# A two-layer trunk of attention and MLP blocks on one core: layer norms by ScalarE, gains in transposed form, and the next stage's first 512 columns by halves of the tokens

## The chip, the cores and the metric

One core of a Trainium2 chip runs the whole program. The metric is device time in microseconds, from a launch to its end. Engines: TensorE (PE in the rows; PEld is its loading of weights), VectorE (DVE), ScalarE (ACT), GpSimd (POOL), and SyncE (SP), whose queue issues most transfers.

## What is computed

256 tokens of 2048 features pass through two layers, each an attention block and an MLP, each followed by a layer norm over a scaled residual:

```python
def layer_norm(x, g, b):
    mu = mean(x); var = mean((x - mu) ** 2)
    return (x - mu) * rsqrt(var + 1e-5) * g + b

def sq_relu_mlp(x, w1, w2):
    return square(relu(x @ w1)) @ w2

for layer in range(2):
    if layer == 0: mix = fox_attention(h, ...)       # 16 heads, forget gates
    else:          mix = nsa_attention(h, ..., *kv)  # compressed, selected and window branches
    h = layer_norm(ALPHA * h + mix, ln1_g[layer], ln1_b[layer])
    h = layer_norm(ALPHA * h + sq_relu_mlp(h, ...), ln2_g[layer], ln2_b[layer])
    if layer == 0: kv = shared_kv(h, kv_w, ...)      # 6 blocks of 512 columns
```

The weights are float32, 419 MB of them in the stream; 2048 by 8192 and back in each MLP, 2048 by 2048 for the attention's projections.

## The kernel before

**Layout.** `h` holds the tokens on partitions: two halves t = 0, 1 of 128 tokens, by 2048 columns; `c` or `n` is a block of 512 of them. A product needs its input with the features on partitions, so each norm's result is transposed on TensorE (L376, 128x128 at a time, into a PSUM tile `pt`) and copied out into `act` chunks.

**Float32 in two parts.** Each operand is split into a hi part, rounded to fp32r (a cast on ScalarE, L117), and a lo part, the remainder (a subtraction on VectorE, L118); a product takes hi x hi, hi x lo and lo x hi. `wload` brings 0.5 MB of weights into a `raw` tile (four of them) and splits it into a `whl` tile of 128 x 2 x 1024 (five of them). `fill_split` does the same for activations.

**Two forms of product.** The column form (`ws_many`, called by `ws_stream`) has 128 output features on partitions and all 256 tokens in a row: for each column j and each of 16 feature blocks one matmul 512 wide (L158, hi weights by hi and lo tokens) and one 256 wide (L160, lo weights by hi tokens). The row form (`xs_mm`, called by `xs_part`) has 128 tokens on partitions and 512 columns in a row, three matmuls 512 wide for each feature block and half (L182). MLPs read `w1` in the column form and `w2` in the row form; projections out of attention use the row form.

**Stages and handovers.** Fox attention, its output projection and norm 0; MLP 0 and norm 1; the shared kv blocks and NSA attention, its projection and norm 2; MLP 1 and norm 3, which is the output. Between a norm and the next product lies a handover, three of them: into MLP 0, into the kv blocks, into MLP 1. `out_proj` does the blocks n = 0 to 2 and hands back `end`, which does the last one. There the last LATE = 4 weight tiles are held in a pool `late`, so that all of t = 0's held matmuls (24) run before t = 1's (24). `done` adds a finished block to `h` (L248 or L250) and takes its statistics (L252). `scalars` makes mean and 1/sqrt(var) out of them in small VectorE operations (L321 to L328) around one square root on ScalarE (L324); L330 is for the last norm alone.

**The norm.** `gained` subtracts the mean and multiplies by the gains (L348), `columns` multiplies by 1/sqrt(var) and adds the bias (L363), both on VectorE in pieces of 256 columns, with gains and biases spread over all partitions (`lng`, `lnb`, 1 MB each, loaded into `late`). `transposer` transposes and splits. While t = 1's chain runs, TensorE does WARM = 14 dummy matmuls (L423) at the second and third handover; at the first it makes tables for the NSA stage (`tables`, L597 and L600) instead. What follows the chain stands inside `tc.issue_after(last)`: every engine gets it behind `last`, the final one of t = 1's scalars, in its order. The last norm has two of its pieces on ScalarE (L354) and GpSimd (L355, L356).

The next stage then begins in the column form, with three columns together in MLP 0, MLP 1 and the kv stream (`together` = 3), so that feature blocks can be multiplied as they come. The order of the instructions on each engine is worked out when the kernel is built, from the order of the code, priorities and the tiles that are free; TensorE, VectorE and ScalarE each work off their own list, and a transfer on SP waits for its tile.

Of the kernel before, what the change touches and what calls it, by code (L numbers as in the profile page):

```python
# [14 lines left out]
OP = mybir.AluOpType  # L15
# [17 lines left out]
LATE = 4  # L33
WARM = 14
# [64 lines left out]
def _trunk(nc, tc, i, out, ctx):  # L99
# [91 lines left out]
    def merge(dst, acc, scale=1.0):  # L191

        t = sp.tile([P, S], F32, tag="mt", name="mt")
# [41 lines left out]
    def out_proj(src, acts, first, ln=None, two=False, between=()):  # L235
# [41 lines left out]
        def end(late, meanwhile=None):  # L277

            ln.gains(late)
            accs = [acc_tile(), acc_tile()]  # L280
            ahead = 8 - LATE
# [5 lines left out]
            ws = [wload(src[3, k // 2], k % 2, late, LATE) for k in range(ahead, 8)]  # L287
            for t in range(2):
# [12 lines left out]
            elif not ln.final:  # L301
                warm(WARM, ws[0][:, 0, :P], ws[0][:, 0, :512])
            with tc.issue_after(last):
                for t, c in ln.rest:
                    ln.columns(t, c)
                if after:
                    after()
        return end

    class Norm:  # L310


        def __init__(self, li, use, final=False):
            self.li, self.use, self.sc, self.had, self.final = li, use, {}, set(), final
            self.early = (2, 3, 0, 1) if final else (0,)
            self.rest = ((1, 3), (1, 0), (1, 1), (1, 2)) if final else (
                (1, 0), (0, 1), (1, 1), (0, 2), (1, 2), (0, 3), (1, 3))

        def scalars(self, t):
# [8 lines left out]
            end = nc.vector.tensor_mul(rstd, y, a)  # L328
            if self.final:
                end = nc.vector.scalar_tensor_tensor(a, mean, -1.0, rstd, op0=OP.mult, op1=OP.mult)  # L330
# [3 lines left out]
        def gains(self, pool):  # L334
            self.gb = []
            for name in ("lng", "lnb"):
                x = pool.tile([P, D], F32, name=name, bufs=1)
# [3 lines left out]
        def pieces(self, t, c):  # L341
            n = 512 if self.final else 256
            return [[x[:, a:a + n] for x in (h[:, t], *self.gb)] for a in range(c * 512, (c + 1) * 512, n)]

        def gained(self, t, c):
            self.had.add((t, c))
            for hs, g, _ in self.pieces(t, c):
                nc.vector.scalar_tensor_tensor(hs, hs, self.sc[t][0], g, op0=OP.subtract, op1=OP.mult)  # L348

        def columns(self, t, c):  # L350
            mean, rstd, nmr = self.sc[t]
            if self.final and (c == 3 or (t, c) == (0, 2)):
                hs, g, b = (x[:, c * 512:(c + 1) * 512] for x in (h[:, t], *self.gb))
# [6 lines left out]
            if (t, c) not in self.had:  # L360
                self.gained(t, c)
            for hs, _, b in self.pieces(t, c):
                nc.vector.scalar_tensor_tensor(hs, hs, rstd, b, op0=OP.mult, op1=OP.add)  # L363
            self.use(t, c)
            if self.final and (t, c) == self.rest[-1]:
                self.use(1, 3)

    def transposer(cs):

        def use(t, c):  # L370
            if not cs:
                cs.extend(act_chunk() for _ in range(4))
            tp = pt_tile()
            for k in range(4):
                f = c * 512 + k * P
                nc.tensor.transpose(tp[:, k * P:(k + 1) * P], h[:, t, f:f + P], eye)  # L376
            for k in (0, 2):
                hi, lo = (cs[c][:, k:k + 2, n, t * P:(t + 1) * P] for n in range(2))
                fill_split(hi, lo, tp[:, k * P:(k + 2) * P].rearrange("p (k t) -> p k t", k=2))
        return use  # L380
# [4 lines left out]
    def mlp(layer, acts, ln):  # L385
        for q in range(4):
            hid = []

            def use(j, acc):
                if j % 4 == 0:  # L390
                    hid.append(act_chunk())
                u = sp.tile([P, S], F32, tag="mu", name="mu")
# [4 lines left out]
            ws_stream([i["w1"][layer, q * 16 + j] for j in range(16)], acts, use, 3 if q == 0 else 1)  # L397
            end = out_proj(i["w2"][layer, q], hid, q == 0, ln if q == 3 else None)
        with tc.tile_pool(name="late", bufs=2) as late:
            end(late)  # L400
# [16 lines left out]
    cb = cp.tile([P, 2, NC, H], F32, name="cb")  # L417

# [21 lines left out]
    def forget_gates():  # L440

        f = sp.tile([P, 5, 2, H], F32, name="f", bufs=1)
# [16 lines left out]
    def gate_sums():  # L459
# [8 lines left out]
        cr_sb = sp.tile([H, S], F32, name="cr", bufs=1)  # L468
# [3 lines left out]
    with tc.tile_pool(name="fp", bufs=2) as fp:  # L472
# [75 lines left out]
        for hg in range(G):  # L548
# [10 lines left out]
            if hg == 0:  # L559
                load(cst, i["cst"])  # L560
                load(bfb, i["bf"].to_broadcast([P, H]))
                gates_end()
# [22 lines left out]
        end = out_proj(i["fo"], oc, True, Norm(0, transposer(xs)), True, [lambda k=k: run(k) for k in range(n, n + 3)])  # L585

    with tc.tile_pool(name="late", bufs=2) as late:
# [23 lines left out]
        end(late, tables)  # L611
    acts, xs = xs, []
    mlp(0, acts, Norm(1, transposer(xs)))


    with tc.tile_pool(name="np", bufs=2) as np_:
# [22 lines left out]
        raws = ap.tile([P, 2, G, S], F32, tag="act", name="rawT")  # L639

        def use_raw(j, acc):
            merge(raws[:, j // G, j % G, :], acc)

        ws_stream([i["kvT"][s, g] for s in range(2) for g in range(G)], xs, use_raw, 3)
        gates_end = narrow(i["ng"], 3 * H, xs, C["s48"], gate)

        def windows(s):
            t = ap.tile([P, NB, 60], F32, tag="act", name="win")
            src = raws[:, s]
# [89 lines left out]
        def plain_v(s, steps=()):  # L739
            accs = [acc_tile(), acc_tile()]  # L740
            for kc in range(4):
                xs_part(i["kvN"][s, kc], xs[kc], accs, kc == 0, kc == 3)
                if kc < len(steps):
                    steps[kc]()
# [185 lines left out]
```

## Time and profile before

| | us |
|---|---|
| median of 3 runs | 2247.69 |
| lowest and highest | 2247.38, 2249.09 |
| the profiled execution, its own time | 2248.41 |
| its span, from the first to the last instruction | 2246.6 |

TensorE's mean granted clock in that execution is 0.995 of full speed. The span is what the trace shows; about 1.8 us lie around it. A row of the timeline gives a start, a duration, the engine, the line, the operation and how many instructions are merged in it; in brackets the idle time ahead of it and what ended that. Matmuls overlap in their pipeline, so time per matmul is read from one start to the next, not from the durations. Times are in microseconds from the start of the span.

### The profile page before, as it was taken

The page shows a single profiled execution, that of the slowest core. Times are in us where ns is not written, and L with a number is a line of the kernel's source. Part 1 is how long each engine was busy: PE and PEld are TensorE (multiplying, and loading weights), DVE is VectorE, ACT ScalarE, POOL GpSimd, SP SyncE. Part 2 cuts the span into 40 slices and gives each one's busy share as a digit, 9 for nine tenths or more (in the row PEclk, how much of TensorE's full clock was granted, in tenths as well). Part 3 has the DMA queues.
Part 4 walks back from the last instruction along what each step waited for, and adds up shares of the span by engine and source line. Part 5 has one row for each costly group of instructions (what it writes and reads, how often), then busy time and mean ns, then how long its engine had stood idle before and what let it go on. Part 6 is the DMA issues. An engine that isn't in the chain of part 4 may idle for free.

```text
span 2246.6 us, 30144 instructions
## 1 busy us (share of the span) xinstructions
PE 2220.6 (99%) x11478; PEld 1893.7 (84%) x11478; DVE 1408.0 (63%) x2209; ACT 1048.2 (47%) x1564; POOL 18.6 (1%) x26
## 2 busy tenths in 40 slices
PE   9999999999999999999999999999999999999997
PEld 6888888888888888888788899888888888888885
DVE  5665556864665565565786688768655645655655
ACT  4444444443444454454355567544434434444542
POOL 0000000000000000000000000000000000000001
PEclk9999999999999999999999999999999999999999
DMA  7665567566666666666556744565666666666663
GB/s 253 196 197 188 178 188 249 198 190 192 192 191 192 193 188 195 190 188 194 179 165 221 246 134 137 168 217 170 192 192 190 191 193 194 189 193 191 189 196 112
DMA packets 116829, 427.54 MB, mean 190 GB/s; under 512 B 13179, under 2 KB 13339, under 8 KB 115406
## 3 DMA queue, kind: packets, MB, share of 16 engines
q1 hardware_dynamic: 114734, 419.00, 59.5%
q0 software_dynamic: 1952, 6.63, 1.0%
q8 instruction: 90, 1.47, 0.3%
q14 instruction: 53, 0.43, 0.1%
HBM read 423.45 MB, written 4.24 MB: 190 GB/s over the span
## 4 chain that ended last, share of the span: by engine, by line
PE 95%; DVE 2%; DMA 2%; ACT 0%; issue 0%; SPq 0%; ACTq 0%; DVEq 0%
PE acc L182 44%; PE acc L158 31%; PE acc L160 16%; DMA raw<-in_fq 1%; PE pt L839 1%; PE lg L775 0%; PE pt L817 0%; PE pt L376 0%; DMA raw<-in_fv 0%; DVE whl L118 0%; DMA bc<-c_dram 0%; DVE h L363 0%; PE acc L692 0%; PE pt L840 0%; PE pt L533 0%; PE lg L771 0%
## 5 line engine op out<-in xcount | busy, mean ns | idle before, releaser
L118 DVE TENSOR_TENSOR whl<-raw,whl 128x1024 fp32r<-128x1024 f32 (+1 forms) x769 | 938.4, 1223 | 613.6 <-ACT whl L117 605.0
L117 ACT CAST whl<-raw 128x1024 fp32r<-128x1024 f32 (+1 forms) x769 | 805.1, 1048 | 740.3 <-PE acc L182 491.6
L182 PE MATMUL acc<-whl,act 128*128 128x512 f32 x4416 | 1011.7, 390 | 2.2 <-DVE whl L118 1.2
L182 PEld LDWEIGHTS acc<-whl,act 128*128 128x128 f32 x4416 | 827.1, 188 | 177.6 <-DVE whl L118 2.8
L158 PE MATMUL acc<-act,whl 128*128 128x512 f32 x3072 | 757.3, 394 | 0.0
L158 PEld LDWEIGHTS acc<-act,whl 128*128 128x128 f32 x3072 | 563.5, 189 | 107.3 <-issue 0.2
L160 PEld LDWEIGHTS acc<-act,whl 128*128 128x128 f32 x3072 | 398.2, 191 | 16.9 <-DVE whl L118 0.3
L160 PE MATMUL acc<-act,whl 128*128 128x256 f32 x3072 | 408.7, 284 | 0.0
L194 ACT ACTIVATE mt<-acc 128x256 f32<-128x256 f32 x192 | 73.4, 382 | 299.7 <-PE acc L158 297.5
L196 DVE TENSOR_TENSOR mu<-acc,mt 128x256 f32<-128x256 f32 x128 | 54.4, 425 | 113.4 <-ACT mt L194 113.4
L394 DVE SCALAR_TENSOR_TENSOR mu<-mu 128x256 f32<-128x256 f32 x128 | 54.4, 425 | 4.3
L118 DVE TENSOR_TENSOR act<-mu,act 128x256 fp32r<-128x256 f32 x128 | 53.7, 420 | 0.0
L117 ACT CAST act<-mu 128x256 fp32r<-128x256 f32 x128 | 52.1, 407 | 3.1 <-DVE mu L394 1.6
L117 ACT CAST act<-pt 128x256 fp32r<-128x256 f32 x80 | 29.4, 372 | 41.9 <-PE pt L376 31.3
L250 DVE TENSOR_TENSOR h<-h,acc 128x512 f32<-128x512 f32 x48 | 30.9, 681 | 14.2 <-PE acc L182 14.2
L118 DVE TENSOR_TENSOR act<-pt,act 128x256 fp32r<-128x256 f32 x80 | 33.1, 419 | 9.9 <-ACT act L117 9.6
L404 ACT ACTIVATE E<-E,sm 128x128 f32<-128x128 f32 (+1 forms) x64 | 28.9, 453 | 7.8 <-DVE sm L407 7.4
L363 DVE SCALAR_TENSOR_TENSOR h<-h,mv,lnb 128x256 f32<-128x256 f32 (+1 forms) x53 | 26.5, 541 | 0.1
L404 ACT ACTIVATE E<-L,sm 128x128 f32<-128x128 f32 (+1 forms) x32 | 14.3, 449 | 24.8 <-DVE sm L407 24.8
L376 PE MATMUL pt<-cst,h 128*128 128x128 f32 x96 | 19.1, 293 | 6.0 <-DVE h L363 6.0
L348 DVE SCALAR_TENSOR_TENSOR h<-h,mv,lng 128x256 f32<-128x256 f32 (+1 forms) x53 | 25.0, 502 | 0.0
L248 DVE SCALAR_TENSOR_TENSOR h<-h,acc 128x512 f32<-128x512 f32 x32 | 20.6, 681 | 4.2 <-PE acc L182 4.2
(173 smaller groups left out, 664.0 us busy)
## 6 DMA issues: line engine op xcount, KB each, us to landing
raw<-in_w SPq DMA_DIRECT2D x512, 512.0 KB, 3.6
raw<-in_fq SPq DMA_DIRECT2D x32, 512.0 KB, 3.7
raw<-in_fk SPq DMA_DIRECT2D x32, 512.0 KB, 3.6
raw<-in_fo SPq DMA_DIRECT2D x32, 512.0 KB, 4.0
raw<-in_kvT SPq DMA_DIRECT2D x32, 512.0 KB, 4.4
raw<-in_nq SPq DMA_DIRECT2D x32, 512.0 KB, 3.7
raw<-in_no SPq DMA_DIRECT2D x32, 512.0 KB, 4.1
raw<-in_fv SPq DMA_DIRECT2D x31, 512.0 KB, 3.7
```

The source lines that it names most:

```text
L117: nc.scalar.copy(hi, src)
L118: nc.vector.tensor_sub(lo, src, hi.bitcast(F32))
L158: mm(acc, w[:, 0, s], a, start=kt == 0, stop=kt == KT - 1)
L160: mm(acc[:, :S], w[:, 1, s], a[:, 0, :], start=False, stop=False)
L182: mm(acc, l, w[:, r, s], start=first and n == 0, stop=last and n == 2)
L194: nc.scalar.activation(t, acc[:, S:], AF.Copy, scale=scale)
L196: nc.vector.tensor_add(dst, acc[:, :S], t)
L250: nc.vector.tensor_add(hcols(t, n), hcols(t, n), acc)
L348: nc.vector.scalar_tensor_tensor(hs, hs, self.sc[t][0], g, op0=OP.subtract, op1=OP.mult)
L363: nc.vector.scalar_tensor_tensor(hs, hs, rstd, b, op0=OP.mult, op1=OP.add)
L394: nc.vector.scalar_tensor_tensor(u, u, 0.0, u, op0=OP.max, op1=OP.mult)
L404: nc.scalar.activation(E, L, AF.Exp, bias=m, scale=-1.0, accum_out=sums)
```

## The change

- LATE is 6 (5 at the first handover), and the dummy matmuls are gone. `end` takes `start`, which does the first 512 columns of the next stage.
- A class `Turned` takes the place of Norm at the three handovers. Its norm is one ScalarE operation of 128x512 (scale 1/sqrt(var), bias -mean/sqrt(var), so L333 now ends the scalars at each norm). Four transposes follow, then gains and biases, which are now one number for each partition (`lnT`, a new small input), in pieces of 128x128 that go by turns to VectorE (`tensor_scalar`, L389) and ScalarE (L387), into a tile `lx`; then the split.
- `first_columns` multiplies those 512 columns in the row form, piece by piece: (t, c) in the order (0,0), (0,1), (1,0), (0,2), (1,1), (0,3), (1,2), (1,3), with weights `w1r` (a row-form copy of w1's first 512 columns) in the MLPs and the value block `kvN[0]` ahead of the NSA stage.
- In the MLPs the result of these columns stands with tokens on partitions, so relu and square are followed by 8 transposes (`turn`) in each. `ws_stream` goes on from column 4, one at a time.
- `residual` makes h * g + b for the residual path later, beside the second column of the stream: 8 VectorE operations of 128x1024 at each handover, with `lng` and `lnb` loaded into `act` tiles at that point.
- The tiles mt and mu have one buffer, and the compress steps of the NSA stage stand among the halves of `kvN[1]`.

```diff
-LATE = 4
-WARM = 14
+LATE = 6
...
             for t in range(2):
                 for kt in range(2 * ahead, KT):
                     xs_mm(accs[t], acts[kt // 4], kt % 4, t, ws[kt // 2 - ahead], False, kt == KT - 1)
...
                 if t == 0:
                     for c in ln.early:
                         ln.columns(0, c)
-                elif not ln.final:
-                    ln.gained(1, 0)
             after = None
             if meanwhile:
                 after = meanwhile()
-            elif not ln.final:
-                warm(WARM, ws[0][:, 0, :P], ws[0][:, 0, :512])
...
             with tc.issue_after(last):
-                for t, c in ln.rest:
-                    ln.columns(t, c)
-                if after:
-                    after()
+                use = start(lambda t, c: ln.columns(t, c) if (t, c) not in ln.had else None)
+            if after:
+                after()
+            return use
...
+    class Turned(Norm):
+        final = False
+        early = (0, 1)
...
+        def columns(self, t, c):
+            if not self.cs:
+                self.cs.extend(act_chunk() for _ in range(4))
+            self.had.add((t, c))
+            _, rstd, nmr = self.sc[t]
+            hs = hcols(t, c)
+            nc.scalar.activation(hs, hs, AF.Identity, bias=nmr, scale=rstd)
+            tp = pt_tile()
+            for k in range(4):
+                nc.tensor.transpose(tp[:, k * P:(k + 1) * P], hs[:, k * P:(k + 1) * P], eye)
+            x = sp.tile([P, 4, P], F32, tag="lx", name="lx")
+            for k in range(4):
+                g, b = (lnT[:, self.li, n, 4 * c + k:4 * c + k + 1] for n in range(2))
+                src = tp[:, k * P:(k + 1) * P]
+                if k % 2:
+                    nc.scalar.activation(x[:, k], src, AF.Identity, bias=b, scale=g)
+                else:
+                    nc.vector.tensor_scalar(x[:, k], src, g, b, op0=OP.mult, op1=OP.add)
+            fill_split(*(self.cs[c][:, :, n, t * P:(t + 1) * P] for n in range(2)), x)
+
+        def residual(self):
+            self.gains(ap, tag="act")
+            for t in range(2):
+                for a in range(0, D, HALF):
+                    hs, g, b = (x[:, a:a + HALF] for x in (h[:, t], *self.gb))
+                    nc.vector.tensor_mul(hs, hs, g)
+                    nc.vector.tensor_add(hs, hs, b)
+
+    def first_columns(src, cs):
+
+        def start(piece):
+            accs = [acc_tile(), acc_tile()]
+            ws = {}
+            for t, c in ((0, 0), (0, 1), (1, 0), (0, 2), (1, 1), (0, 3), (1, 2), (1, 3)):
+                piece(t, c)
+                if c not in ws:
+                    ws[c] = [wload(src[c], k) for k in range(2)]
+                for kt in range(4):
+                    xs_mm(accs[t], cs[c], kt, t, ws[c][kt // 2], c == 0 and kt == 0, c == 3 and kt == 3)
+            return accs
+        return start
...
-            ws_stream([i["w1"][layer, q * 16 + j] for j in range(16)], acts, use, 3 if q == 0 else 1)
+            if q == 0:
+                us = []
+                for t in range(2):
+                    u = sp.tile([P, 512], F32, tag="lx", name="fu")
+                    nc.scalar.activation(u, accs[t], AF.Relu)
+                    nc.vector.tensor_mul(u, u, u)
+                    us.append(u)
+                hid.append(act_chunk())
+
+                def use0(j, acc):
+                    if j == 0:
+                        for t in range(2):
+                            turn(t, us[t])
+                    use(j, acc)
+                    if j == 1:
+                        before.residual()
+
+                ws_stream([i["w1"][layer, j] for j in range(4, 16)], acts, use0)
...
+        "w1r": np.stack([rows(w[:, :512])[0] for w in a["mlp_w1"]]),
...
+        "lnT": np.stack([ln_g[:3], ln_b[:3]], 1).reshape(3, 2, KT, P).transpose(3, 0, 1, 2),
```

Most line numbers move by one in the changed kernel (L182 is L181 there, L118 is L117, L158 is L157), and L376 becomes L381.

TensorE's list at the second handover, out of MLP 0 into the kv blocks, in the kernel before (`acc` is a block's sum, `pt` the transposed columns, `idle` the dummies' output):

```order
L182 MATMUL acc<-whl,act 128x512 x377
L376 MATMUL pt<-cst,h 128x128 x4
L182 MATMUL acc<-whl,act 128x512 x7
L423 MATMUL idle<-whl 128x512 x14
L376 MATMUL pt<-cst,h 128x128 x8
L158 MATMUL acc<-act,whl 128x512 x8
L160 MATMUL acc<-act,whl 128x256 x2
L376 MATMUL pt<-cst,h 128x128 x2
```

The same place on TensorE in the changed kernel:

```order
L381 MATMUL pt<-cst,h 128x128 x4
L181 MATMUL acc<-whl,act 128x512
L381 MATMUL pt<-cst,h 128x128 x4
L181 MATMUL acc<-whl,act 128x512 x19
L381 MATMUL pt<-cst,h 128x128
L181 MATMUL acc<-whl,act 128x512 x23
L381 MATMUL pt<-cst,h 128x128 x11
L181 MATMUL acc<-whl,act 128x512 x2
L381 MATMUL pt<-cst,h 128x128 x3
L181 MATMUL acc<-whl,act 128x512 x34
L381 MATMUL pt<-cst,h 128x128 x5
L157 MATMUL acc<-act,whl 128x512 x8
```

The dummies are gone, t = 0's first eight transposes stand ahead of the last 18 held matmuls, and the next stage's first block (L181) stands in four pieces among the transposes. The 18 and the first matmul of the next stage make up the 19. The third handover has the same rows but for 13 in place of 19.

VectorE's list at the same handover, behind t = 1's last statistics, in the kernel before (`mv` holds the scalars, `whl` weights, `act` the split columns):

```order
L321 BN_AGGR mv<-stats 128x2
L323 TENSOR_SCALAR mv<-mv 128x1
L348 SCALAR_TENSOR_TENSOR h<-h,mv,lng 128x256
L325 RECIPROCAL mv<-mv 128x1
L348 SCALAR_TENSOR_TENSOR h<-h,mv,lng 128x256
L326 SCALAR_TENSOR_TENSOR mv<-mv 128x1
L327 TENSOR_SCALAR mv<-mv 128x1
L328 TENSOR_TENSOR mv<-mv 128x1
L348 SCALAR_TENSOR_TENSOR h<-h,mv,lng 128x256
L363 SCALAR_TENSOR_TENSOR h<-h,mv,lnb 128x256 x2
```

The same place on VectorE in the changed kernel:

```order
L325 BN_AGGR mv<-stats 128x2
L327 TENSOR_SCALAR mv<-mv 128x1
L329 RECIPROCAL mv<-mv 128x1
L330 SCALAR_TENSOR_TENSOR mv<-mv 128x1
L331 TENSOR_SCALAR mv<-mv 128x1
L332 TENSOR_TENSOR mv<-mv 128x1
L333 SCALAR_TENSOR_TENSOR mv<-mv 128x1
L117 TENSOR_TENSOR whl<-raw,whl 128x1024 x5
L389 TENSOR_SCALAR lx<-pt,lnT 128x128 x4
L117 TENSOR_TENSOR act<-lx,act 128x4x128
```

The gains are gone from among the scalars, L333 has come on, and the lo halves of five weight tiles stand between it and t = 1's first pieces; the first four belong to the feature blocks (0,0) and (0,1) of the next stage.

## Rows read from the trace of the kernel before

**Rows 1.** The page: busy time, share and instructions of each engine.

```profile
PE 2220.6 (99%) x11478; PEld 1893.7 (84%) x11478; DVE 1408.0 (63%) x2209; ACT 1048.2 (47%) x1564; POOL 18.6 (1%) x26
```

**Rows 2.** Timeline of TensorE, first handover: start, duration, engine, line, operation, [idle before].

```profile
397.87 0.82 PE L597 MATMUL rps<-oh 99*16 99x384 f32 x2
398.62 2.43 PE L600 MATMUL cbps<-oh 99*128 99x48 f32 x20
403.68 1.12 PE L376 MATMUL pt<-cst,h 128*128 128x128 f32 x4 [2.64 <-DVE h L363]
...
405.72 2.73 PE L158 MATMUL acc<-act,whl 128*128 128x512 f32 x8
408.29 0.40 PE L160 MATMUL acc<-act,whl 128*128 128x256 f32 x2
408.52 0.38 PE L376 MATMUL pt<-cst,h 128*128 128x128 f32 x2
...
408.87 0.38 PE L376 MATMUL pt<-cst,h 128*128 128x128 f32 x2
```

**Rows 3.** Timeline of TensorE, second handover.

```profile
1114.27 3.37 PE L423 MATMUL idle<-whl 128*128 128x512 f32 x14
...
1120.50 3.65 PE L158 MATMUL acc<-act,whl 128*128 128x512 f32 x8
1123.99 0.40 PE L160 MATMUL acc<-act,whl 128*128 128x256 f32 x2
```

**Rows 4.** Timeline of TensorE, third handover.

```profile
1516.10 3.38 PE L423 MATMUL idle<-whl 128*128 128x512 f32 x14
...
1522.80 3.43 PE L158 MATMUL acc<-act,whl 128*128 128x512 f32 x8
1526.03 0.63 PE L160 MATMUL acc<-act,whl 128*128 128x256 f32 x2
```

**Rows 5.** Stretches: length, busy time of PE, PEld, DVE, ACT, POOL, clock, DMA.

```profile
403.70:405.70 2.00, 1.84 (x8) 1.26 (x8) 1.97 (x6) 0.37 (x1) 0.00 (x0) 0.50 0.96 309
...
1120.50:1122.50 2.00, 2.00 (x6) 1.61 (x6) 1.90 (x6) 1.02 (x3) 0.00 (x0) 0.50 0.00 0
```

**Rows 6.** Timeline of VectorE, second handover, t = 1's chain.

```profile
1114.47 0.69 DVE L250 TENSOR_TENSOR h<-h,acc 128x512 f32<-128x512 f32 x1
...
1117.14 0.21 DVE L326 SCALAR_TENSOR_TENSOR mv<-mv 128x1 f32<-128x1 f32 x1
...
1117.58 0.16 DVE L328 TENSOR_TENSOR mv<-mv 128x1 f32<-128x1 f32 x1
```

**Rows 7.** Groups by line and form: count, busy us, mean ns, idle before.

```profile
L118 DVE TENSOR_TENSOR whl<-raw,whl 128x1024 fp32r<-128x1024 f32 x767 | 937.0, 1224 | 611.5 <-ACT whl L117 602.9
L117 ACT CAST whl<-raw 128x1024 fp32r<-128x1024 f32 x767 | 803.8, 1049 | 738.1 <-PE acc L182 491.6 <-PE acc L160 164.7 <-issue 32.2
...
L802 DVE TENSOR_SCALAR E<-E,sm 128x128 f32<-128x128 f32 x32 | 9.0, 281 | 0.0
...
L820 ACT COPY PT<-pt 128x128 f32<-128x128 f32 x32 | 8.5, 267 | 14.9 <-DVE PT L118 14.9
...
L354 ACT ACTIVATE h<-h,mv 128x512 f32<-128x512 f32 x3 | 2.3, 810 | 4.7 <-DVE mv L330 4.7
...
L117 ACT CAST act<-raw 128x512 fp32r<-128x512 f32 x2 | 1.2, 618 | 1.8 <-DMA raw<-in_xT 1.8
```

**Rows 8.** Timeline of TensorE in MLP 0's stream: one column pair of L158.

```profile
429.21 3.82 PE L158 MATMUL acc<-act,whl 128*128 128x512 f32 x16
432.86 1.35 PE L160 MATMUL acc<-act,whl 128*128 128x256 f32 x10
```

**Rows 9.** Timeline at the end of the span: t = 1's scalars beside GpSimd.

```profile
2234.13 1.05 DVE L326 SCALAR_TENSOR_TENSOR mv<-mv 128x1 f32<-128x1 f32 x1
...
2235.24 1.26 POOL L356 TENSOR_TENSOR h<-h,lnb 128x512 f32<-128x512 f32 x1
2235.41 1.12 DVE L328 TENSOR_TENSOR mv<-mv 128x1 f32<-128x1 f32 x1
```

More of the change, by code (lines that the diff above doesn't have):

```diff
@@ L275, in out_proj, with end @@
                 ended(n, accs)
-        def end(late, meanwhile=None):
-            ln.gains(late)
+        def end(late, start=None, meanwhile=None, held=LATE):
+            if ln.final:
+                ln.gains(ap, tag="act")
             accs = [acc_tile(), acc_tile()]
-            ahead = 8 - LATE
+            ahead = 8 - held
             for k in range(ahead):
@@ L286, in end @@
                         xs_mm(accs[t], acts[k // 2], kt, t, w, k == 0 and kt == 0, False)
-            ws = [wload(src[3, k // 2], k % 2, late, LATE) for k in range(ahead, 8)]
+            ws = [wload(src[3, k // 2], k % 2, late, held) for k in range(ahead, 8)]
             for t in range(2):
@@ L359, in columns @@
                 return
[L360 to L363, printed above, removed]
+            nc.vector.scalar_tensor_tensor(hs, hs, mean, g, op0=OP.subtract, op1=OP.mult)
+            nc.vector.scalar_tensor_tensor(hs, hs, rstd, b, op0=OP.mult, op1=OP.add)
             self.use(t, c)
-            if self.final and (t, c) == self.rest[-1]:
+            if (t, c) == self.rest[-1]:
@@ L584, in _trunk @@
         xs = []
-        end = out_proj(i["fo"], oc, True, Norm(0, transposer(xs)), True, [lambda k=k: run(k) for k in range(n, n + 3)])
+        ln = Turned(0, xs)
+        end = out_proj(i["fo"], oc, True, ln, True, [lambda k=k: run(k) for k in range(n, n + 3)])
     with tc.tile_pool(name="late", bufs=2) as late:
@@ L609, in tables @@
             return keep_them
-        end(late, tables)
+        accs = end(late, first_columns(i["w1r"][0], xs), tables, LATE - 1)
     acts, xs = xs, []
-    mlp(0, acts, Norm(1, transposer(xs)))
+    ln, before = Turned(1, xs), ln
+    accs = mlp(0, acts, accs, before, ln, first_columns(i["kvN"][0], xs))
     with tc.tile_pool(name="np", bufs=2) as np_:
@@ L637, in bands, with keep_v @@
             return bass.AP(tensor=t.tensor, offset=t.offset, ap=[*[list(x) for x in t.ap[:-1]], [32, 3], [1, NC]])
-        raws = ap.tile([P, 2, G, S], F32, tag="act", name="rawT")
-        def use_raw(j, acc):
-            merge(raws[:, j // G, j % G, :], acc)
-        ws_stream([i["kvT"][s, g] for s in range(2) for g in range(G)], xs, use_raw, 3)
+        def keep_v(s, accs):
+            fill_split(vhl[:, s, 0, :], vhl[:, s, 1, :], accs[0])
+            nc.scalar.copy(v1[:, s, :], accs[1])
+        keep_v(0, accs)
+        raws = []
+        def use_raw(j, acc):
+            if j == 0:
+                raws.append(ap.tile([P, 2, G, S], F32, tag="act", name="rawT"))
+            merge(raws[0][:, j // G, j % G, :], acc)
+            if j == 1:
+                ln.residual()
+        ws_stream([i["kvT"][s, g] for s in range(2) for g in range(G)], xs, use_raw)
         gates_end = narrow(i["ng"], 3 * H, xs, C["s48"], gate)
@@ L737, in compress @@
             return hidden, end
[L739 to L744, printed above, removed]
-            fill_split(vhl[:, s, 0, :], vhl[:, s, 1, :], accs[0])
-            nc.scalar.copy(v1[:, s, :], accs[1])
-        plain_v(0, compress(0))
-        cmp_v = compress(1)
-        plain_v(1, cmp_v)
+        accs = [acc_tile(), acc_tile()]
+        for s in range(2):
+            steps = compress(s)
+            for k in range(2):
+                kc = 2 * s + k
+                xs_part(i["kvN"][1, kc], xs[kc], accs, kc == 0, kc == 3)
+                steps[k]()
+        keep_v(1, accs)
         oc = []
@@ L859, in _trunk @@
         acts = []
-        end = out_proj(i["no"], oc, True, Norm(2, transposer(acts)), True, [lambda k=k: run(k) for k in range(n, n + 4)])
+        ln = Turned(2, acts)
+        end = out_proj(i["no"], oc, True, ln, True, [lambda k=k: run(k) for k in range(n, n + 4)])
     with tc.tile_pool(name="late", bufs=2) as late:
-        end(late)
-    mlp(1, acts, Norm(3, to_output, True))
+        accs = end(late, first_columns(i["w1r"][1], acts))
+    mlp(1, acts, accs, ln, Norm(3, to_output))
 def laid_out(a):
```

70 lines of the change are left out of this document (34 added, 36 removed).

## The prediction

> **What bounds the kernel now.** I read the page first: TensorE is busy for 2220.6 of 2246.6 us [rows 1], so only its 26 us of idle time and its slow stretches can be won; a microsecond on another engine counts only where TensorE waits for it. Next I read TensorE's timeline at the three handovers that the change rewrites, from the last held matmul of one stage to the first matmul of the next, and worked out the time in which TensorE does no useful work.
>
> First handover [rows 2]: the held matmuls end at 397.87 and L158 begins at 405.72, which is 7.85. In it lie useful table products (L597 and L600, until about 401.0: 3.13) and 8 transposes. A transpose takes about 0.115: from 408.52 to 408.87 stand two of them and one L160, and an L160 takes 0.115 (408.29 to 408.52 for two). So 7.85 - 3.13 - 0.92 = 3.80 is lost. Then the 8 L158 take 408.29 - 405.72 = 2.57, where 16 of them elsewhere take 432.86 - 429.21 = 3.65, or 0.228 each [rows 8], 1.83 for eight: 0.74 more. Second handover [rows 3]: 1120.50 - 1114.27 - 0.92 = 5.31 (the L423 are dummies), and 3.49 - 1.83 = 1.66. Third [rows 4]: 6.70 - 0.92 = 5.78, and 3.23 - 1.83 = 1.40. The slow matmuls are explained by the granted clock, which is at half (0.50), the 1.2 GHz level, right after the idle stretch of the first two [rows 5]. Lost in all: 4.54 + 6.97 + 7.18 = **18.69**. That is all that the new handovers could win.
>
> What TensorE waits for there is the chain of the second half of the tokens (t=1): accumulate, statistics, scalars, gains. At the second handover it runs from 1114.47 to 1117.74 on VectorE [rows 6].
>
> **The change, part by part.** The intent of the new order is that TensorE multiplies the first half's columns (0,0) and (0,1) while t=1's chain runs. The listing of TensorE's order says otherwise. At the second handover, behind the 19 matmuls that end t=1's held products and begin the next stage, stands one L381 alone, and the 23 matmuls follow it. 18 of the 19 are held ones; the one other is the first of (0,0). That L381 transposes (1,0), so it needs t=1's norm, thus its whole chain. TensorE works its instructions off in order, so the 23 matmuls queue behind it. They would wait anyhow: VectorE's list has the lo halves of their weights (L117, 128x1024) behind t=1's last scalar, L333.
>
> *First wait.* Counted from the last held matmul at the second handover: 0.20 to L250, 3.27 to the end of L328 [rows 6], less 0.25 for the two L348 that no longer stand between, plus 0.20 for the new L333, 0.81 for the norm on ScalarE (L354's row, [rows 7]) and 0.1 of hand-over (estimate): 4.33. One matmul is done in it: 4.33 - 0.23 = 4.1. The lo halves come at 1.22 each [rows 7] from L333 on, so the first is there some 0.3 after the norm and the next three just keep pace with six matmuls each: 4.3 lost. For the third handover, whose lists read alike, I take the same. At the first, the table products stay in front: the wait's end stood 403.68 - 397.87 = 5.81 behind the held matmuls [rows 2]; 0.81 + 0.20 for norm and L333 come on, one L363 of some 0.43 goes: 6.39, less 3.13 of tables = 3.26.
>
> *Clock.* TensorE idles for about as long as before, now without the dummies in it, so I let the clock fall in all three: 1.66 each (the second handover's own price).
>
> *Second wait.* After the 23 come 11 transposes, three of (1,0) first; the matmuls of (1,0) wait for its pieces, which VectorE and ScalarE make in turns on one tile: two tensor_scalars of 0.28 (L802's row), two ScalarE pieces of 0.27 (L820's row) and one of the neighbouring tile between them, then a hi copy of 0.62 [rows 7], together 2.26 without hand-overs. Eight transposes cover 0.92: 1.35 lost. Bounds: 0.8 if no neighbour gets between, 2.2 with slower pieces.
>
> *Reload.* The fifth weight tile of the ring is freed by (1,1); the next column needs a new one, whose hi cast takes 1.05 [rows 7] against 5 transposes of 0.58: with hand-over 0.57, and 0.33 estimated for the pieces of (1,1) and (1,2). 0.9; bounds 0 and 2.
>
> *First half's transposes.* They stand after 17 of the 30 held matmuls of t=1, so 3.9 us after t=0's end, against a chain of 4.3: 0.3 at the second and third handover, none at the first, where 23 stand ahead.
>
> Sum of the handovers: 3.26 + 1.66 + 1.35 + 0.9 = 7.2, and twice 4.3 + 1.66 + 1.35 + 0.9 + 0.3 = 8.5, in all 24.2. Against 18.69 that is **+5.5**.
>
> *Other terms.* Eight more transposes in each of two MLPs: 16 x 0.115 = +1.8. Four columns in row form are 96 matmuls of 0.228 = 21.9, against 4 x (16 x 0.228 + 16 x 0.115) = 22.0: -0.1 each, -0.2 in all (the kvN block was in row form already). The residual's 8 VectorE operations of 128x1024 (1.22 each, L118's row) lie beside matmuls at the second and third handover, with weights between them; at the first all eight stand in one row, 9.8 us, against a ring of five tiles of some 2.8 us: +0.5, between 0 and 6. The larger load of gains now stands behind the next stage's weights on SP, and costs nothing by the ring's lead. The tail: t=1's L326 and L328 take 1.05 and 1.12 while GpSimd's L356 runs [rows 9], against 0.21 and 0.16 undisturbed [rows 6]. With 6 held tiles for 4, t=1 ends 12 x 0.228 = 2.7 later against t=0's chain, when GpSimd is done: -1.8. The small new load at the start: +0.1. Together +0.4.
>
> By this the change costs 5.5 + 0.4 = 5.9 in the profiled execution: 2248.41 + 5.9 = 2254.3. That execution lies 0.7 above the median of the runs shown, so the forecast is 2253.6. The estimates lean high at the reload, which the bound 0 can take away at the first handover, so I set **2253.0**.
>
> *Where a rule and a row differ.* The nearest row to the new 128x128 ScalarE pieces is a copy out of PSUM of 0.27 [rows 7]; they read two pointers besides. The Trainium skill ("ScalarE: Activation LUTs", section "What ACT_TABLE_LOAD costs") gives 186 ns plus 0.833 ns an element, and some 93 ns for each [128,1] pointer operand. L354's row, 0.81 with two pointers, agrees with it (0.80). By the page such a piece would take an estimated 0.48, and three of them in the (1,0) chain would make that wait 0.6 longer at each handover, 1.9 in all: 2254.9. The same page's "Rules for kernel authors" advise VectorE for mul and add, which speaks against the norm and the pieces on ScalarE.
>
> **The rivals.** (A) *The clock holds, so the result is not slower.* If TensorE's idle stretches don't bring the clock down, 3 x 1.66 = 5.0 goes: 2248.0. If the pieces are quick too, so that second wait and reload shrink to their lower bounds, another 3 x 0.55 + 3 x 0.9 = 4.4 goes: 2243.6. It decides at a stretch of idle time that the clock survives. For it: before, 8 transposes lay between the idle stretch and the slow matmuls, now there is one. Against it: it fell at all three handovers of before ([rows 5], and 8 L158 in 3.23 us at the third, [rows 4]), after less idling than 4 us.
>
> (B) *It falls a second time*, behind the lull of 11 transposes and a wait of 1.35: 3 x 1.66 = 5.0 more, 2258.0. Against it: matmuls run for some 6 us between the waits.
>
> (C) *The weights run dry behind the residual*, at its upper bound of 6 us at the first handover: 2259. Against it: VectorE is needed for only 1.22 of each 2.8 us by the stream.
>
> (D) *The change does what it is laid out to do*: the 23 matmuls cover the chain. Then the first wait of 4.3 (3.26) and its clock loss go nearly whole, some 15 us, 2238. Only an engine that passes a waiting matmul would allow that, and the lo halves stand behind L333 all the same. I give it 4 in 100.
>
> **How the numbers follow.** A measurement of this kernel tells some 0.2%, 4.5 us, from no change: slower begins at 2252.2, faster ends at 2243.2. Forecast 0.52, within 2249 to 2257, three fifths of it slower (0.31), the rest same (0.21). A 0.24: same 0.15, faster 0.08, 0.01 slower. B 0.11 and C 0.09 slower, D 0.04 faster. Faster 0.12, same 0.36, slower 0.52. The range runs from 2244 to 2260: it leaves out the lowest tenth (D and the end of A) and the upper end of C.
>
> **What would show it.** In the timeline after: one L181 and an idle stretch of some 4 us before the lone L381 at the second and third handover, released by ScalarE's norm; then L181 at the half clock; a wait of over 1 us behind the 11 transposes; L326 at 0.2 in the tail. It is wrong if L181 fills t=1's chain, if the granted clock stays at 1.00 through the handovers, or if L118's successor (L117) leaves TensorE waiting beside the residual.

## The result, and the profile after

| | before, us | after, us |
|---|---|---|
| median | 2248.18 (4 runs) | 2265.80 (4 runs) |
| lowest and highest | 2247.38, 2249.09 | 2263.24, 2268.98 |
| profiled execution, own time | 2248.41 | 2263.24 |
| its span | 2246.6 | 2261.5 |

The ratio is 1.0079 (interval 1.0061 to 1.0096): the change costs some 18 us, three times the forecast, and lies above its range. The profiled execution is the quickest of the four, 14.8 above that of before; what follows explains these 14.8. The other 2.8 us of the difference between the medians are in no trace.

TensorE after, first handover (compare [rows 2]; columns as there):

```profile
397.18 0.82 PE L659 MATMUL rps<-oh 99*16 99x384 f32 x2
397.93 2.43 PE L662 MATMUL cbps<-oh 99*128 99x48 f32 x20
400.18 0.47 PE L181 MATMUL acc<-whl,act 128*128 128x512 f32 x1
404.01 0.90 PE L381 MATMUL pt<-cst,h 128*128 128x128 f32 x3 [3.35 <-ACT h L378]
404.56 7.37 PE L181 MATMUL acc<-whl,act 128*128 128x512 f32 x23
411.77 0.71 PE L381 MATMUL pt<-cst,h 128*128 128x128 f32 x5
417.88 1.97 PE L381 MATMUL pt<-cst,h 128*128 128x128 f32 x8 [5.40 <-ACT lx L387]
419.50 12.51 PE L181 MATMUL acc<-whl,act 128*128 128x512 f32 x48
431.85 1.03 PE L381 MATMUL pt<-cst,h 128*128 128x128 f32 x8
432.64 2.09 PE L157 MATMUL acc<-act,whl 128*128 128x512 f32 x8
```

One L181, 3.35 of waiting for ScalarE's norm (L378) at a group of three L381, then the 23: the order that the prediction read from the lists. Behind the next L381 stands a second wait, for ScalarE's pieces (L387), and it is 5.40, not 1.35. It stands ahead of transposes, not of the matmuls of (1,0) as the prediction had it: there are two `pt` tiles, and the third group of four transposes after the norm has to wait until the pieces have read the first tile. Second handover (compare [rows 3]):

```profile
1119.66 4.61 PE L181 MATMUL acc<-whl,act 128*128 128x512 f32 x19
1128.21 0.33 PE L381 MATMUL pt<-cst,h 128*128 128x128 f32 x1 [3.93 <-ACT h L378]
1128.49 7.10 PE L181 MATMUL acc<-whl,act 128*128 128x512 f32 x23
1135.43 0.93 PE L381 MATMUL pt<-cst,h 128*128 128x128 f32 x7
1137.86 0.66 PE L381 MATMUL pt<-cst,h 128*128 128x128 f32 x4 [1.50 <-ACT lx L387]
...
1148.56 2.11 PE L157 MATMUL acc<-act,whl 128*128 128x512 f32 x8 [0.59 <-ACT whl L116]
```

Here all three waits are near the forecast: 3.93 for 4.1 to 4.3, 1.50 for 1.35, and 0.59 for the reloaded weight tile (forecast 0.9). The third handover (compare [rows 4]) reads the same:

```profile
1535.33 0.48 PE L381 MATMUL pt<-cst,h 128*128 128x128 f32 x1 [4.36 <-ACT h L378]
1535.62 6.81 PE L181 MATMUL acc<-whl,act 128*128 128x512 f32 x23
1542.27 0.93 PE L381 MATMUL pt<-cst,h 128*128 128x128 f32 x7
1544.69 0.66 PE L381 MATMUL pt<-cst,h 128*128 128x128 f32 x4 [1.50 <-ACT lx L387]
```

At 0.228 each, 23 matmuls take 5.24; they took 7.21, 6.94 and 6.65 from start to start. The granted clock says why, and shows a second fall at the first handover and none at the second (stretches; columns as in [rows 5]):

```profile
404.00:408.00 4.00, 3.99 (x11) 3.32 (x12) 3.64 (x4) 2.07 (x3) 0.00 (x0) 0.50 1.04 334
...
416.00:420.00 4.00, 2.12 (x9) 2.10 (x10) 2.76 (x8) 2.70 (x6) 0.00 (x0) 0.50 0.46 151
420.00:424.00 4.00, 4.00 (x14) 3.13 (x13) 1.35 (x5) 1.81 (x4) 0.00 (x0) 0.72 0.00 0
...
1128.00:1132.00 4.00, 3.79 (x10) 2.92 (x11) 3.85 (x4) 2.28 (x4) 0.00 (x0) 0.60 0.76 247
...
1140.00:1148.00 8.00, 7.96 (x38) 6.22 (x36) 4.51 (x6) 4.73 (x7) 0.00 (x0) 1.00 0.44 132
```

In the first of these the DMA share is 1.04: the 16 DMA engines are busy throughout. Why the second wait at the first handover is so long stands on ScalarE and VectorE, from the norm on (timelines of the two):

```profile
403.14 2.93 ACT L378 ACTIVATE h<-h,mv 128x512 f32<-128x512 f32 x4 [1.56 <-DVE mv L333]
413.77 1.04 ACT L116 CAST whl<-raw 128x1024 fp32r<-128x1024 f32 x1 [7.70 <-DMA raw<-in_w1r]
416.43 1.77 ACT L387 ACTIVATE lx<-pt,lnT 128x128 f32<-128x128 f32 x4 [1.61 <-DVE lx L389]
```

```profile
402.94 0.16 DVE L333 SCALAR_TENSOR_TENSOR mv<-mv 128x1 f32<-128x1 f32 x1
403.02 4.62 DVE L117 TENSOR_TENSOR whl<-raw,whl 128x1024 fp32r<-128x1024 f32 x4
414.85 1.22 DVE L117 TENSOR_TENSOR whl<-raw,whl 128x1024 fp32r<-128x1024 f32 x1 [7.21 <-ACT whl L116]
415.99 0.72 DVE L389 TENSOR_SCALAR lx<-pt,lnT 128x128 f32<-128x128 f32 x2
```

ScalarE stands 7.70 us before the cast of a weight tile that has not landed, and its pieces for (1,0) are queued behind that cast; VectorE stands 7.21 before the lo half of the same tile, with L389 behind it. The transfer was issued late (timeline of SP's queue), and ran beside another one (DMA issues of 398 to 420: size, time to landing):

```profile
404.30 4.26 SPq L113 DMA_DIRECT2D raw<-in_w1r  x4
```

```profile
b_dram<-r_dram POOLq DMA_DIRECT2D x1, 2048.0 KB, 12.6
raw<-in_w1r SPq DMA_DIRECT2D x4, 512.0 KB, 9.7
```

These four w1r weights were issued from 404.30 on. Raw tiles number four, all four held c = 0 and 1, and they came free as L117 finished with them (the first at about 404.2), which was behind L333. So the fence, `tc.issue_after` behind t = 1's last scalar L333, holds back the next weights as well as the 23 matmuls, into the 12.6 us of the table's 2 MB (`b_dram`, the spread bias table of the NSA stage). Before, SP issued no weights between 390 and 419, so the table had these transfers to itself and met nobody who waited.

A further loss is in the NSA stage, at the second of the two compress products (L764): four waits for weights, 0.73 + 0.52 + 0.29 + 0.52 = 2.06, where before the only wait in that stretch is 0.20 (TensorE after):

```profile
1276.21 3.67 PE L764 MATMUL acc<-whl,winhl 128*120 128x512 f32 x12 [0.73 <-DVE whl L117]
1280.39 1.19 PE L764 MATMUL acc<-whl,winhl 128*120 128x512 f32 x4 [0.52 <-DVE whl L117]
1281.88 0.74 PE L181 MATMUL acc<-whl,act 128*128 128x512 f32 x2 [0.29 <-ACT whl L116]
1283.14 5.27 PE L181 MATMUL acc<-whl,act 128*128 128x512 f32 x22 [0.52 <-DVE whl L117]
```

### The profile page after: what moved, and what is told of

Read it like the earlier page. It is cut to its first block, busy times and chain, and to the rows that moved or that the text cites. A ratio compares the mean times of both kernels' runs of the same rounds, so it can differ in the third digit from the quotient of the medians.

```text
span 2261.5 us, 30078 instructions
## 1 busy us (share of the span) xinstructions
PE 2220.3 (98%) x11402; PEld 1889.4 (84%) x11402; DVE 1405.8 (62%) x2151; ACT 1080.4 (48%) x1604; POOL 18.6 (1%) x26
## 4 chain that ended last, share of the span: by engine, by line
PE 93%; DMA 3%; DVE 3%; ACT 1%; issue 0%; SPq 0%; ACTq 0%; DVEq 0%
PE acc L181 45%; PE acc L157 28%; PE acc L159 15%; DVE whl L117 1%; PE pt L907 1%; PE pt L885 0%; PE lg L843 0%; DMA lnb<-in_lnb 0%; DMA raw<-in_cw 0%; DMA bc<-c_dram 0%; PE pt L381 0%; DMA raw<-in_w1r 0%; DVE h L398 0%; ACT whl L116 0%; PE acc L764 0%; PE acc L207 0%
## 5 line engine op out<-in xcount | busy, mean ns | idle before, releaser
L117 DVE TENSOR_TENSOR whl<-raw,whl 128x1024 fp32r<-128x1024 f32 (+1 forms) x769 | 937.9, 1223 | 603.0 <-ACT whl L116 594.4
L181 PE MATMUL acc<-whl,act 128*128 128x512 f32 x4608 | 1064.8, 392 | 2.3 <-DVE whl L117 1.3
L181 PEld LDWEIGHTS acc<-whl,act 128*128 128x128 f32 x4608 | 866.8, 189 | 187.1 <-DVE whl L117 3.1
L157 PE MATMUL acc<-act,whl 128*128 128x512 f32 x2944 | 718.8, 393 | 1.2 <-ACT whl L116 1.2
L157 PEld LDWEIGHTS acc<-act,whl 128*128 128x128 f32 x2944 | 538.8, 188 | 104.8 <-ACT whl L116 1.7
L159 PEld LDWEIGHTS acc<-act,whl 128*128 128x128 f32 x2944 | 378.9, 191 | 16.5 <-DVE whl L117 1.7
L159 PE MATMUL acc<-act,whl 128*128 128x256 f32 x2944 | 387.0, 283 | 0.7 <-DVE whl L117 0.5
L117 DVE TENSOR_TENSOR act<-mu,act 128x256 fp32r<-128x256 f32 x120 | 50.1, 418 | 0.0
L381 PE MATMUL pt<-cst,h 128*128 128x128 f32 x96 | 15.9, 295 | 20.3 <-ACT h L378 11.9
L381 PEld LDWEIGHTS pt<-cst,h 128*128 128x128 f32 x96 | 12.2, 150 | 24.2 <-ACT h L378 13.5
L387 ACT ACTIVATE lx<-pt,lnT 128x128 f32<-128x128 f32 x48 | 20.8, 455 | 16.3 <-DVE lx L389 16.0
L389 DVE TENSOR_SCALAR lx<-pt,lnT 128x128 f32<-128x128 f32 x48 | 18.8, 407 | 13.9 <-PE pt L381 10.7
L466 DVE CUSTOM_DVE_ANT_0 E<-lg,nbm 128x128 f32<-128x128 f32 (+1 forms) x64 | 22.4, 350 | 0.2
```

The costliest lines, as they stand in the source:

```text
L117: nc.vector.tensor_sub(lo, src, hi.bitcast(F32))
L157: mm(acc, w[:, 0, s], a, start=kt == 0, stop=kt == KT - 1)
L159: mm(acc[:, :S], w[:, 1, s], a[:, 0, :], start=False, stop=False)
L181: mm(acc, l, w[:, r, s], start=first and n == 0, stop=last and n == 2)
L381: nc.tensor.transpose(tp[:, k * P:(k + 1) * P], hs[:, k * P:(k + 1) * P], eye)
```

## The experiments

Theory F (fence): what matters is which instructions stand behind t = 1's last scalar. Rival S (ScalarE): the norm and the pieces in their new place and form are what costs. Beside them C (collision with the table) and R (the ring of five `whl` tiles runs short at the compress products). Times are medians, beside the kernel before on the same chip.

**early.** The first two pieces' weights and matmuls ahead of the fence.

```diff
             for n, (t, c) in enumerate(((0, 0), (0, 1), (1, 0), ...)):
+                if n == 2:
+                    yield accs
...
                 if t == 0:
                     for c in ln.early:
                         ln.columns(0, c)
+                    go = start(...)
+                    next(go)
...
             with tc.issue_after(last):
-                use = start(...)
+                use = next(go)
```

> Edit: the weights and matmuls of (0,0) and (0,1) are issued ahead of t=1's held products and outside the fence behind t=1's scalars; all else as in the changed kernel. Theory F (the fence): the lo halves of these weights stand behind L333, so TensorE waits for them (3.35, 3.93 and 4.36 us at the three handovers) and their raw tiles come free late, so the next weights land late and ScalarE's cast of them holds up the pieces of (1,0) (5.40, 1.50, 1.50). It expects the first waits gone, the second wait at the first handover under 2, the half clock gone with them: about 20 us less than the changed kernel, some 2246. Theory S (ScalarE: the norm and the 128x128 pieces there are what is slow): the second waits stay at 5.4, 1.5, 1.5, and only the first waits go: some 2254.

Measured: 2247.71 against 2247.70, ratio 1.0002 (0.9993 to 1.0012): 18 us less than the changed kernel, where F expects about 20 and S 12. At the first and third handover the first wait is gone and the second is 1.49 and 1.62. At the second handover a wait was left:

```profile
1109.08 9.97 PE L181 MATMUL acc<-whl,act 128*128 128x512 f32 x42
1123.22 1.97 PE L384 MATMUL pt<-cst,h 128*128 128x128 f32 x8 [4.17 <-ACT h L381]
```

There the list had the next stage's 24 matmuls ahead of the last six held ones, so t = 1's chain began only behind all 42. The table still spreads at its old place in this run, and the second wait of the first handover is short all the same: all eight w1r weights of MLP 0 were issued before 390 and don't meet it.

**turned_only** and **first_only**: the two halves of the change, each alone.

```diff
 turned_only:
-                use = start(lambda t, c: ln.columns(t, c) if (t, c) not in ln.had else None)
+                for t, c in ((1, 0), (0, 2), (1, 1), (0, 3), (1, 2), (1, 3)):
+                    ln.columns(t, c)
...
-                ws_stream([i["w1"][layer, j] for j in range(4, 16)], acts, use0)
+                ws_stream([i["w1"][layer, j] for j in range(16)], acts, use0, 3)
...
 first_only:
-LATE = 6
+LATE = 4
...
-            nc.scalar.activation(hs, hs, AF.Identity, bias=nmr, scale=rstd)
+                nc.vector.scalar_tensor_tensor(hs, hs, mean, g, op0=OP.subtract, op1=OP.mult)
+                nc.vector.scalar_tensor_tensor(hs, hs, rstd, b, op0=OP.mult, op1=OP.add)
...
```

> Edit: the norm on ScalarE, the gains in transposed form and the later residual stay; the next stage begins as in the kernel before, in the column form with three columns together, and the compress steps stand as before. Theory F: no weights of the next stage hang on the fence in a new way, so this lies near the kernel before: the chain of about 4.5 us and a piece chain of some 2 us at each handover, no dummies: 2248 to 2256. Theory S: the pieces stay the bottleneck and it lies nearer to the changed kernel, 2258 to 2266.

> Edit: the first 512 columns in the row form by halves of the tokens, fence and all, but the norm, gains and biases on VectorE as in the kernel before (256-column pieces, gains in the late pool, 4 held tiles, no later residual). Theory F: lo halves and raw tiles still hang behind t=1's scalars, so it loses about as much as the changed kernel: 2260 to 2268. Theory S: without ScalarE's pieces it is near the kernel before: 2247 to 2253.

Measured: turned_only 2253.07 (1.0025, 1.0014 to 1.0036), first_only 2258.45 (1.0051, 1.0035 to 1.0068). The norm in its new form, with no dummies and an unchanged start, costs some 5, inside F's band; the first columns behind the fence cost 11 with VectorE's own norm. That falls 1.5 short of F's band and lies 5.5 above S's. So both halves of the change cost time; S is wrong that the norm costs most of it. The second handover of first_only shows the fence without ScalarE in it:

```profile
1116.45 0.94 PE L181 MATMUL acc<-whl,act 128*128 128x512 f32 x3
1122.30 7.57 PE L181 MATMUL acc<-whl,act 128*128 128x512 f32 x23 [4.91 <-DVE whl L117]
```

Here TensorE waits at the 23 for VectorE's lo half, the wait that the prediction named as standing behind the first ("they would wait anyhow"). Even without the lone L381 it costs 4.91.

**latebd.** The 2 MB spread moved away from the handover.

```diff
-                nc.gpsimd.dma_start(b_dram, bass.AP(tensor=r_dram.tensor, ...))
...
+                if layer == 0 and q == 1 and j == 4:
+                    with tc.issue_after(queue[-1]):
+                        load(b_dram, bass.AP(tensor=r_dram.tensor, ...))
```

> Edit: the 2 MB spread of the bias table (b_dram) is issued in the second quarter of MLP 0 instead of at the first handover; all else as in the changed kernel. Theory C (collision): the weights of (0,2) took 9.6 us to land at the first handover because this transfer ran beside them; without it they land in about 4, the second wait there falls from 5.40 to about 1.5, and the time by 4 to 6 us, to some 2260, and the spread from run to run shrinks. If the late issue alone is the cause, the wait stays over 4 and the time within 2 us of 2265.8.

Measured: 2261.94 (1.0067, 1.0052 to 1.0082), 3.9 less, a little under the forecast 4 to 6; the interval overlaps that of the changed kernel, so the time alone settles nothing. The trace does. The same weights, issued at the same place, land in 5.1:

```profile
raw<-in_w1r SPq DMA_DIRECT2D x4, 512.0 KB, 5.1
```

```profile
414.06 1.16 PE L381 MATMUL pt<-cst,h 128*128 128x128 f32 x8 [1.50 <-ACT lx L387]
415.07 11.26 PE L181 MATMUL acc<-whl,act 128*128 128x512 f32 x48
```

The second wait is 1.50, as at the other handovers, and the 48 matmuls run at the full clock (426.17 - 415.07 = 11.1; 12.35 in the changed kernel). The handover as a whole, from L659 to L157, takes 426.96 - 397.58 = 29.38 instead of 35.46: 6.1 less. Most of it comes back in the profiled execution, which with 2264.42 is 1.2 above that of the changed kernel. In MLP 0 TensorE waits 2.83 once for weights behind the table on SP's queue, which this edit brought there:

```profile
618.98 3.02 PE L157 MATMUL acc<-act,whl 128*128 128x512 f32 x8 [2.83 <-ACT whl L116]
```

At the second handover it is only 1.2 ahead (its first L381 at 1117.36 for 1118.55), and at the third the 23 matmuls take 8.32 for 6.65; why they take longer is open. For the second wait C holds, together with the late issue: either without the other leaves 1.5 (early, latebd, and the other two handovers). What the collision is worth in the whole time is not shown.

**early2**, **early2_c3**, **first_early2**, **warm**.

```diff
 early2, against early: behind t = 1's held products
+                if t and start:
+                    go = start(...)
+                    next(go)
                 done(3, t, accs[t])
                 last = ln.scalars(t)
 early2_c3: three parts of kvN[1] between the compress products
+        steps = compress(0)
+        part(0)
+        steps[0]()
+        part(1)
+        steps[1]()
+        part(2)
+        steps = compress(1)
+        part(3)
+        steps[0]()
...
+        at(0, steps[1])
 first_early2: first_only with the edit of early2
 warm, against the changed kernel:
+            if not meanwhile:
+                warm(14, ws[0][:, 0, :P], ws[0][:, 0, :512])
```

> Edit: as in the run early, but the weights and matmuls of (0,0) and (0,1) are issued behind t=1's held products, still ahead of its scalars, so that at the second handover all 18 held matmuls stand ahead of the 24 of the next stage (in early, 24 stood ahead of the last six, and 4.17 us of waiting were left there). Theory F: the last first wait goes, with the half clock behind it: 5 to 6 us less than early, 2241 to 2243, faster than the kernel before by 0.2 to 0.3 per cent. If something else held the norm up there, the wait stays and the time is that of early, 2247.7.

> Edit: early2, and in the NSA stage three of the four feature blocks of kvN[1] between the two compress products instead of two, so that the weight ring has more time to fill. Theory R (ring): the waits of 2.06 us for weights at the second compress product in the changed kernel (1.6 in early) come from reordering the compress steps, which take a weight tile in 0.9 us where the row form takes 2.7; they shrink to under 0.5: 1 to 2 us less than early2. If the waits come from elsewhere: no change.

> Edit: the first 512 columns by halves with weights ahead of the fence, as in early2, but the norm, gains and biases on VectorE as in the kernel before (the run first_only without the fence). Theory F: it gains nearly as much against first_only (2258.5) as early2 against the changed kernel: 2243 to 2249. Theory S (ScalarE's norm and pieces cost time in themselves) expects it to be faster than early2, under 2241; if the norm in transposed form brings something of its own, it is slower than early2 by 2 or more.

> Edit: the changed kernel with the 14 dummy matmuls of the kernel before put back behind t=1's held products at the second and third handover. If the half clock there (23 matmuls in 6.94 and 6.65 us instead of 5.24) comes from TensorE idling through the first wait, the dummies lift it to the full clock for these matmuls, and 1.4 to 1.7 us are won at each of the two: 3 us less than the changed kernel. If the transposes and the wait alone set it, the 23 matmuls still take over 6.5.

early2: 2241.14 against 2247.29, ratio 0.9971 (0.9960 to 0.9982), as F forecast. The second handover is now one run of matmuls:

```profile
1108.98 9.85 PE L181 MATMUL acc<-whl,act 128*128 128x512 f32 x42
1118.67 1.03 PE L384 MATMUL pt<-cst,h 128*128 128x128 f32 x8
1121.20 0.66 PE L384 MATMUL pt<-cst,h 128*128 128x128 f32 x4 [1.50 <-ACT lx L390]
```

42 L181 in 9.69 are 0.231 each: the full clock, and t = 1's chain under 24 useful matmuls.

early2_c3: 2238.90, ratio 0.9964 (0.9951 to 0.9978), the quickest of the study and faster than both kernels. Its waits at the compress products are 0.55 and 0.25, where early2 has 0.79, 0.25 and 0.53; another at L810 goes from 1.42 to 0.24. The 0.80 left is more than the 0.5 that R allows, so R holds in part. turned_only supports it: there the compress steps stand as before, four feature blocks between the two products, and no wait for weights is left in that stretch. The intervals of the two times overlap, so the 2.2 us between the medians are not settled.

first_early2: 2240.46, ratio 0.9971 (0.9959 to 0.9983), 18 less than first_only. That is 2.5 below F's band, which was too high, and inside S's "under 2241". But S wants it faster than early2, and the two differ by nothing that can be measured. So once the weights stand ahead of the fence, no difference between the two forms of the norm is seen.

warm: a single run, 2258.79. The first waits shrink to 0.69 and 1.18 behind the dummies, and the 23 matmuls take 5.34 at both places; at the first handover, which got no dummies, they still take 6.85. The second handover:

```profile
1122.88 3.35 PE L485 MATMUL idle<-whl 128*128 128x512 f32 x14
1126.06 0.40 PE L181 MATMUL acc<-whl,act 128*128 128x512 f32 x1
1127.15 0.55 PE L383 MATMUL pt<-cst,h 128*128 128x128 f32 x3 [0.69 <-ACT h L380]
1127.45 5.50 PE L181 MATMUL acc<-whl,act 128*128 128x512 f32 x23
1132.79 0.71 PE L383 MATMUL pt<-cst,h 128*128 128x128 f32 x5
1136.27 1.10 PE L383 MATMUL pt<-cst,h 128*128 128x128 f32 x8 [2.77 <-ACT lx L389]
```

So the half clock behind the first wait comes of TensorE's idling in it, and costs 1.60 + 1.31 at these two. Dummies alone don't keep the clock up: in the kernel before, the same 14 were followed by waits of 0.94 and 0.44 (at 1118.58 and 1119.86) among eight transposes, and the L158 behind them ran at half clock [rows 5]. Against the gain stands the second wait at the second handover, 2.77 for 1.50. The run is 4.5 below the profiled execution of the changed kernel, more than the 2.9; with a single run the rest is open.

**early2_c3_dve** and **first_early2_c3**.

```diff
-                if k % 2:
-                    nc.scalar.activation(x[:, k], src, AF.Identity, bias=b, scale=g)
-                else:
-                    nc.vector.tensor_scalar(x[:, k], src, g, b, op0=OP.mult, op1=OP.add)
+                nc.vector.tensor_scalar(x[:, k], src, g, b, op0=OP.mult, op1=OP.add)
```

> Edit: early2_c3, with all four 128x128 pieces of a feature block's gains and biases on VectorE (L389's form) instead of by turns with ScalarE. Theory P (the turns): the second wait of 1.50 at each handover is a chain of four pieces that hand a tile back and forth between two engines (0.41 and 0.46 each in the trace, and a hand-over each time); on one engine the four take about 1.6 without hand-overs, the wait shrinks to under 1.2, and the time by about 1 us against early2_c3. If VectorE is the fuller engine there, its lo halves come later and the time rises by 0 to 2.

> Edit: first_early2 with the compress order of early2_c3: the norm as in the kernel before, the first columns by halves with their weights ahead of the fence, three feature blocks between the compress products. If the norm in transposed form is worth nothing once the weights stand ahead of the fence, this lies within 1.5 us of early2_c3, 2237 to 2240; if it is worth something, it is 2 or more slower than early2_c3.

early2_c3_dve: the second wait falls from 1.50, 1.50 and 1.63 in early2_c3 to 1.12, 1.11 and 1.12, as P says, but the time is 2240.19 (0.9965, 0.9952 to 0.9977), no gain: waits of 0.81 beside the residual (0.17 in early2_c3) and 1.05 at the compress products (0.80) stand against it. first_early2_c3: 2239.15 (0.9960, 0.9946 to 0.9973), within 0.3 of early2_c3. With this order too, no difference between the two forms of the norm is seen.

## Why the prediction was wrong

**Right.** The order argument and its prices. First waits: forecast 3.26, 4.3, 4.3; measured 3.35, 3.93, 4.36. The clock behind them: forecast 3 x 1.66 = 5.0; measured 1.97 + 1.70 + 1.41 = 5.1. Second wait at the second and third handover: 1.35 against 1.50 and 1.50; this is in part luck, since the pieces as listed add up to 1.99, not 2.26, which would make the wait 1.07, and since it ends with the pieces and not with the hi copy that the sum has in it. The residual at the first handover: 0.5 against 0.54 (the prediction's own sign of being wrong, L117 keeping TensorE waiting there, thus came true at the size that its sum had). The tail: -1.8; from TensorE's last matmul to the end of the span it took 2246.6 - 2231.7 = 14.9 before and 2261.5 - 2248.5 = 13.0 now, so -1.9. Its rows answer to [rows 9]: L330 took 0.22 and L332 0.16.

**Wrong.** The step *Second wait* priced the first handover like the others: 1.35, with 2.2 as its upper bound, and it was 5.40. I followed the chain of pieces, but not the queue that they stand in: ScalarE's list has the cast of the next weights ahead of them, and that cast waits for a transfer, the transfer for a raw tile, the raw tile for L117, and L117 for L333. VectorE's list has the lo half of that tile ahead of its own pieces in the same way. The prediction had seen the last link ("the lo halves stand behind L333") and drew from it only the wait of the 23 matmuls. The second omission is the table's 2 MB in that window, whose DMA share of 0.96 stood in [rows 5]. Together 4.05 too little; early and latebd each bring this wait down to 1.5.

Rival (B), a second fall of the clock, was priced for all three handovers; it came at the first alone, behind the long wait: 8 L381 in 1.62 for 0.92, and 48 L181 in 12.35 for 10.94, 2.1 in all. The prediction had this second fall at all three handovers or at none; the second waits of 1.50 were not followed by a fall, that of 5.40 was. What length of wait brings one is not shown.

The compress order in the NSA stage is not in the sum at all: +2.06. The change is named in the description; no term was made of it, although a compress product takes a weight tile for every four matmuls (0.9 us) where the row form takes one for twelve (2.7), and although two feature blocks now stand between the two products where four stood.

The *Reload* was too high: 0.59, 0.59 and none at the first handover, 1.2 for 2.7. Counted as the prediction counts, the handovers cost 31.3 (13.3, 9.0, 9.0) instead of 24.2; some 2.6 of that are spread over shorter pieces of the stretches that no single wait shows. With this the sum comes out: 31.3 - 18.69 = 12.6 for the handovers, 2.06 for the compress order and the 0.4 forecast for the other terms make 15.1, for 14.8 measured.

The pieces: L387 took 0.455 and L389 0.407, not 0.27 and 0.28 as the rows of other operations gave. The Trainium skill's estimate for ScalarE ("ScalarE: Activation LUTs", section "What ACT_TABLE_LOAD costs"), 0.48, was the better one. The waits of 1.50 lie only 0.15 above the forecast, not the 0.6 that the prediction worked out from it: at the second handover VectorE's four pieces (1135.96 to 1137.80) and ScalarE's three (1136.41 to 1137.80) run side by side.

Rival (D), that the 23 matmuls cover the chain, failed, as forecast, for this kernel, and early2 shows what it is worth: 24.7 us less than the changed kernel, 2241 for the rival's 2238.

## What to carry to other kernels

What stands behind a fence holds more than the engine that it names: the buffers that those instructions would free, and so the transfers into them, and whatever other engines have queued behind the arrival. When work is meant to cover a chain, read the built order and look for its operands, its casts and its weights as well as its matmuls; here moving four weight tiles and their matmuls ahead of the scalars turned +18 us into -6. A transfer that is hidden in one order is to be looked at again when another order starts its transfers later.

## What was not expected of the hardware

Four 0.5 MB transfers that land in 5.1 us by themselves took 9.7 beside one of 2 MB, and that one took 12.6 where it had taken 10.1 in the kernel before. A ScalarE operation of 128x128 out of PSUM with scale and bias read from pointers took 0.455 us, where a copy of the same shape takes 0.267 [rows 7].
